# Moving the context projection of a second transformer block into the stream of expert weights

## The chip, the cores and the metric

The kernel runs on one core of a Trainium2 chip. It is one program for five engines: TensorE (PE, matrix products; PEld is its loading of weights), VectorE (DVE), ScalarE (ACT), GpSimd (POOL) and SyncE (SP), which here only starts transfers. The metric is the device time of one execution in microseconds (us).

## The reference

Two blocks run one after the other on 512 tokens of width 1024. The first one ends in a mixture of 16 experts, each of which takes 64 tokens; every expert has 24 MiB of weights in float32. The second block takes the normalized result x and a context of 256 tokens:

```python
x = x + ec_moe(rmsnorm(x, norm_ffn_g), router_w, expert_w_gu, expert_w_down)
x = rmsnorm(x, final_norm_g)
# second block; shift, scale, shift_c, scale_c come from c_2 and c_ctx_2
h  = rmsnorm_2(x, norm_g)   * (1 + scale)   + shift
hc = rmsnorm_2(ctx, norm_g) * (1 + scale_c) + shift_c
ckv, kr, kb, vb, cq, za, qb, zb, ga, gb = split_cols(h @ w_in, ...)   # 160 + 512 + 512 + 256 + ... columns
c_ckv, c_kr, c_kb, c_vb = split_cols(hc @ w_in[:, :1184], ...)        # the context projection
```

Then come a latent attention and a neighbourhood attention (tokens lie on 8 rows by 64 columns), both of which also attend to the context, gates, an output product, the residual and a last norm.

## The kernel before

**Experts.** Weights come from `in_expert_w_dram` as 192 ring tiles of [128, 4, 1024] (2 MiB), 12 for each expert, loaded by SP into a ring of nine slots (`Raw`: `first` fills the ring, `load` fetches one tile further each time one has been used). `expert(e, ...)` runs `up` four times and `down` twice. Between its parts it calls generators: `scatter(q)` adds the results of an expert pair to the residual `x` through one-hot matrices from `pick` (a comparison of `iota` with token numbers), `gather(q)` collects the next pair's tokens. For expert 15 the generator is `context()`.

**Before the experts**, `x` is complete after the last addition of the cross attention (L961), and the router takes its top 64 tokens in a chain of DVE instructions; `iota` is written by POOL at L1140, and the first `pick` (L1147) reads it.

**Context.** `context()` loads `ctx_2`, the two rows of gains, the context columns of `w_in_2` (`wkv`, 4 MiB in ring slots 2 and 3, and `wkr`), builds rows of shift and scale for the context and for x (`mod_rows`), normalizes the context (`mod_norm`) and transposes it into `hc`.

**Between the blocks.** After `scatter(7)`, `fin_norm(q)` takes two token tiles of 128 each: squares on ACT (L1418, L1420), the product with a gain (L1419), a Newton iteration of [128, 4] instructions on DVE (L143 to L162, L1423 to L1425), the scaled row h (L1429), the addition of the shift (L1431, one tile on DVE, one on POOL), then x itself is scaled on ACT (L1433). `fin_turn(t)` transposes h on PE and writes it as a high and a low part (L134 ACT, L135 DVE) into `hT`, in another token order (eight columns of the grid together). `ctx_proj(t)` multiplies `hc` by `wkv` and `wkr` and copies out (L1403, L1407). The first product of the second block, `pp`, is 416 columns wide (latent, rope and query latent): four weight units (L228 high part on ACT, L229 low part on DVE or POOL) in the outer loop and four token tiles in the inner one, three matrix products each (L129, L130, L131). `x` is kept in memory as `xd` meanwhile. At the end x comes back, and the output goes out in the plain token order, after `ymT` has been permuted back.

The order of instructions on each engine is set when the program is built, by a scheduler with a model of the times; on the chip each engine takes its queue in order.

Of the kernel before, what the change touches and what calls it, by code (L numbers as in the profile page):

```python
# [68 lines left out]
G_C, G_FFN = 25, 41  # L69
NCOL = 49  # L70
# [7 lines left out]
def body(ctx, tc, a, stop=None, dump=None):  # L78
# [819 lines left out]
    class Raw:  # L898
# [4 lines left out]

        def fetch(self, i):
            r, src = (i - len(self.specs)) % NW, self.specs[i]
            if r:
                w = slot(r, [128, 4, 1024], "we")
                nc.sync.dma_start(w, src)
                self.tiles[i] = [w[:, k] for k in range(4)]
                return  # L910

            self.tiles[i] = []
            for j in range(2):
                w = mid(("r8", "m8")[j], [128, 2, 1024], F32, "we")
                nc.sync.dma_start(w, src[:, 2 * j:2 * j + 2])
                self.tiles[i] += [w[:, 0], w[:, 1]]

        def first(self, r0, r1):
            for r in range(r0, r1):
                self.fetch((r + len(self.specs)) % NW)  # L920
# [6 lines left out]
        def use(self, i):  # L927

            return self.tiles.pop(i)

# [12 lines left out]
    wx = Raw([a["expert_w"][e, i] for e in range(16) for i in range(NT)])  # L943
# [156 lines left out]


# [42 lines left out]
    def pick(q, i):  # L1144

        o = p2("b2", [128, 512], F32R, "ot")
        V.tensor_scalar(o, iota, tokc[:, i, q:q + 1], None, op0=OP.is_equal)  # L1147
        return o

    def gather(q, n=4):  # L1150

        o = pick(q, 0)
# [19 lines left out]
    def scatter(q):  # L1172
        y = Y.pop(q)
        ot = [pick(q, i) for i in range(2)]
# [14 lines left out]
    def expert(e, mid_a, mid_b, half):  # L1189
        q, i = divmod(e, 2)  # L1190
        w0 = NT * e

        def up(j):
            p = ps(tag="gu")
            for k in range(8):
                if k % 4 == 0:
                    w = wx.use(w0 + 2 * j + k // 4)
# [3 lines left out]
                if k % 4 == 3:  # L1201
                    wx.load(w0 + 2 * j + k // 4 + 1 + NW)
# [18 lines left out]
        def down(c, hT, p):  # L1221
            for k in range(8):
                if k % 4 == 0:
                    w = wx.use(w0 + 8 + 2 * c + k // 4)
# [5 lines left out]
                if k % 4 == 3:  # L1230
                    wx.load(w0 + 8 + 2 * c + k // 4 + 1 + NW)
# [27 lines left out]
    def mod_rows(ab, v):  # L1259

        for i in range(2):
            for c in range(2):
                p = ps((128, 2, 256), tag="sc")
                for hf in range(2):
                    r = C_SEL + 32 * hf + 2 * (2 * i + c) + v
                    mm(p[:, hf], cst[:, r:r + 1].to_broadcast([128, 128]), mrow, True, True)
                d = ab[:, i, 512 * c:512 * c + 512]
                p = p.rearrange("p a b -> p (a b)")
                if i == 0:
                    S.activation(d, p, AF.Copy)  # L1270
                else:
                    V.scalar_tensor_tensor(d, p, 1.0, cx["g"][:, 0, 512 * c:512 * c + 512],
                                           op0=OP.add, op1=OP.mult)

    def mod_norm(src, ab, out):

        ss = sm.tile([128, 1], F32, name=nm("ss"), tag="ss1")
        S.activation(out, src, AF.Square, accum_out=ss)
        r = rsqrt(ss, 1024, 1, "mn")
        V.scalar_tensor_tensor(out, src, r, ab[:, 1], op0=OP.mult, op1=OP.mult)  # L1280
        G.tensor_add(out, out, ab[:, 0])

    def context():

        ctx_t = mid("b8", [128, 2, 1024], F32, "ctx")
        nc.sync.dma_start(ctx_t, a["ctx_2"][0].rearrange("(t p) d -> p t d", p=128))
        ga = slot(1, [128, 4, 1024], "gg")
        cx["g"], cx["ab"] = ga[:, 0:2], ga[:, 2:4]
        rows(cx["g"][:, 0], R_G2, 1024)
        rows(cx["g"][:, 1], R_FIN, 1024)  # L1290
        cx["kv"] = []
        for k in range(4):
            if k % 2 == 0:
                w4 = slot(2 + k // 2, [128, 4, 1024], "wkv")
            w = w4[:, 2 * (k % 2):2 * (k % 2) + 2]
            nc.sync.dma_start(w, w_in2[256 * k:256 * k + 256, 160:1184].rearrange("(k p) c -> p k c", p=128))
            cx["kv"].append(w)
        yield 1
        abc = mid("b8", [128, 2, 1024], F32, "abc")
        mod_rows(abc, 1)  # L1300
        mod_rows(cx["ab"], 0)
        yield 1
        hc = cx["hc"] = mid("r8", [128, 8, 256], F32, "hc")
        xn = mid("m8", [128, 2, 1024], F32, "xc")
        for t in range(2):
            mod_norm(ctx_t[:, t], abc, xn[:, t])
        yield 1
        for t in range(2):
            for j0 in (0, 4):
                p = ps((128, 4, 128), tag="tn")  # L1310
                for j in range(4):
                    T.transpose(p[:, j], xn[:, t, (j0 + j) * 128:(j0 + j + 1) * 128], ident)
                S.activation(hc[:, j0:j0 + 4, tsl(t)], p, AF.Copy)
        w = cx["kr"] = mid("m8", [128, 8, 160], F32, "wkr")
        nc.gpsimd.dma_start(w, w_in2[:, 0:160].rearrange("(k p) c -> p k c", p=128))
# [6 lines left out]
    for e in range(NEX):  # L1322
# [24 lines left out]
    p3 = Pool("p3", "left", {"b8": 4, "w4": P3W, "h4": P3H, "b4": 2, "ck": 1})  # L1347
# [45 lines left out]
    ckr = p3("ck", [128, 2, 160], F32, "ckr")  # L1393
    ckb = p3("b4", [128, 2, 512], F32, "ckb")
    cvb = p3("b4", [128, 2, 512], F32, "cvb")

    def ctx_proj(t):
        act = lambda k: cx["hc"][:, k, tsl(t)]
        for i, dst in enumerate((ckb, cvb)):
            p = ps(tag="cx")  # L1400
            for k in range(8):
                mm(p, act(k), cx["kv"][k // 2][:, k % 2, 512 * i:512 * i + 512], k == 0, k == 7)
            S.activation(dst[:, t], p, AF.Copy)  # L1403
        p = ps(tag="cx")
        for k in range(8):
            mm(p[:, :160], act(k), cx["kr"][:, k], k == 0, k == 7)
        S.activation(ckr[:, t], p[:, :160], AF.Copy)  # L1407
# [3 lines left out]
    def fin_norm(q):  # L1411
# [23 lines left out]
    def fin_turn(t):  # L1435
        h = hn2[t // 2][:, t % 2]
        for i in range(2):
# [3 lines left out]
            hh, hl = hT.buf(i)  # L1441
# [11 lines left out]
    xd = ctx.enter_context(tc.tile_pool(name="dram", bufs=1, space=bass.MemoryType.DRAM)).tile(  # L1453
        [128, 4, 1024], F32, name="xd")
# [598 lines left out]
```

## Time and profile before

| | us |
|---|---|
| median of 3 runs (lowest, highest) | 1931.11 (1928.12, 1932.21) |
| the profiled execution, whole | 1936.54 |
| its span in the trace | 1933.6 |

Times in the rows count from the start of the span. In a timeline row stand the start, the duration, the engine, the line, the operation with its output and inputs, a count, and in brackets how long the engine had been idle and what ended that.

### The profile page before, as it was taken

How to read it: one execution, taken by the hardware profiler on the slowest of the kernel's cores; microseconds unless marked ns; L12 is line 12 of the kernel's file. 1: busy time of each engine (PE TensorE's matmuls, PEld its weight loads, DVE VectorE, ACT ScalarE, POOL GpSimd, SP SyncE). 2: the span in 40 equal slices, each digit the busy share in tenths (PEclk: the TensorE clock that was granted, in tenths of full speed). 3: DMA queues.
4: the chain of work that ended last, by engine and by line, in shares of the span. 5: the costliest groups of instructions: out<-in, count | busy, mean ns of one | idle time of the engine just before them, and what ended most of it. 6: DMA issues, size and time to landing. Idle time of an engine off the chain costs nothing.

```text
span 1933.6 us, 24628 instructions
## 1 busy us (share of the span) xinstructions
PE 1750.2 (91%) x10248; PEld 1085.2 (56%) x10248; DVE 681.6 (35%) x1364; ACT 491.5 (25%) x946; POOL 256.1 (13%) x271
## 2 busy tenths in 40 slices
PE   6999999969999898878888798887899999999998
PEld 6975579943433232323323233322487888888778
DVE  6696786540011101001020010101634333554565
ACT  4335543411000000000000000001445444344433
POOL 2371102000000000000000000001213111333351
PEclk9998999979999999999999999999999999999999
DMA  6322623449999999999999999999322202332232
GB/s 213 110 80 85 205 76 95 175 184 409 426 427 425 425 427 426 425 427 426 426 426 426 427 425 425 428 425 416 108 69 61 55 23 58 88 96 82 80 112 85
DMA packets 95870, 493.33 MB, mean 255 GB/s; under 512 B 6484, under 2 KB 56384, under 8 KB 68112
## 3 DMA queue, kind: packets, MB, share of 16 engines
q1 hardware_dynamic: 91008, 475.49, 61.9%
q0 software_dynamic: 3168, 10.45, 1.8%
q10 hardware_dynamic: 1584, 5.83, 0.8%
q8 instruction: 80, 1.31, 0.3%
q14 instruction: 30, 0.25, 0.0%
HBM read 486.50 MB, written 4.19 MB: 254 GB/s over the span
## 4 chain that ended last, share of the span: by engine, by line
PE 47%; DMA 40%; DVE 3%; ACT 1%; issue 1%; POOL 0%; ACTq 0%; SPq 0%; DVEq 0%
DMA we<-in_expert_w_dram 39%; PE ps L126 18%; PE ps L129 8%; PE ps L130 8%; PE ps L131 8%; PE ps L1652 1%; PE ps L1810 1%; PE ps L743 1%; DMA w<-in_w_out_dram 1%; DMA voff<-vb 1%; DVE wl L229 0%; PE ps L1629 0%; PE ps L1216 0%; DVE x L1419 0%; PE ps L1779 0%
## 5 line engine op out<-in xcount | busy, mean ns | idle before, releaser
L126 PE MATMUL ps<-we,xe 128*64 128x512 f32 x2048 | 465.2, 598 | 57.7 <-DMA we<-in_expert_w_dram 57.7
L126 PEld LDWEIGHTS ps<-we,xe 128*64 128x64 f32 x2048 | 143.3, 137 | 346.6 <-issue 258.2
L126 PE MATMUL ps<-we,hT 128*64 128x512 f32 x1024 | 236.3, 604 | 28.3 <-DMA we<-in_expert_w_dram 23.0
L126 PEld LDWEIGHTS ps<-we,hT 128*64 128x64 f32 x1024 | 71.7, 138 | 164.1 <-issue 133.9
L228 ACT ACTIVATE wh<-w 128x1024 fp32r<-128x1024 f32 (+4 forms) x100 | 103.8, 1040 | 122.8 <-PE ps L130 74.0
L1252 DVE SCALAR_TENSOR_TENSOR y<-ps,gate,y 64x512 fp32r<-64x512 f32 x32 | 23.9, 748 | 308.8 <-ACT y L1251 308.8
L1210 DVE TENSOR_TENSOR hid<-hid,ps 128x512 f32<-128x512 f32 x32 | 22.0, 688 | 310.7 <-PE ps L126 291.0
L1218 ACT ACTIVATE hT<-ps 128x512 f32<-128x512 f32 x32 | 19.1, 597 | 430.2 <-PE ps L1216 430.2
L229 POOL TENSOR_TENSOR wl<-w,wh 128x1024 fp32r<-128x1024 f32 (+2 forms) x38 | 90.2, 2375 | 264.3 <-ACT wh L228 241.7
L300 POOL DMA_DIRECT2D gg<-in_rows_dram x2 | 1.1, 560 | 899.0 <-DMA we<-in_expert_w_dram 899.0
L229 DVE TENSOR_TENSOR wl<-w,wh 128x1024 fp32r<-128x1024 f32 (+3 forms) x58 | 77.9, 1344 | 72.3 <-ACT wh L228 71.9
L1251 ACT ACTIVATE y<-ps,gate 64x512 fp32r<-64x512 f32 x32 | 21.8, 682 | 249.5 <-PE ps L126 238.7
L129 PE MATMUL ps<-hTh,wh 128*128 128x512 f32 x192 | 77.3, 403 | 1.6 <-ACT va L1567 1.6
L130 PE MATMUL ps<-hTl,wh 128*128 128x512 f32 x192 | 76.4, 398 | 0.0
L131 PE MATMUL ps<-hTh,wl 128*128 128x512 f32 x192 | 76.1, 397 | 0.0
L126 PEld LDWEIGHTS ps<-otT,xn 128*128 128x128 f32 x512 | 61.0, 196 | 24.6 <-issue 23.6
L129 PE MATMUL ps<-wh,hTh 128*128 128x256 f32 (+1 forms) x224 | 67.1, 299 | 1.2 <-ACT hTh L134 1.0
L126 PE MATMUL ps<-otT,xn 128*128 128x128 f32 x512 | 66.9, 286 | 0.7 <-ACT otT L1157 0.7
L130 PE MATMUL ps<-wl,hTh 128*128 128x256 f32 (+1 forms) x224 | 66.3, 296 | 0.0
L131 PE MATMUL ps<-wh,hTl 128*128 128x256 f32 (+1 forms) x224 | 65.5, 295 | 0.0
L1169 DVE TENSOR_TENSOR xe<-ps,cols 128x512 f32<-128x512 f32 (+1 forms) x18 | 10.2, 598 | 148.9 <-PE ps L126 148.9
L1181 DVE TENSOR_TENSOR x<-x,ps 128x512 f32<-128x512 f32 x64 | 41.8, 685 | 57.7 <-PE ps L126 57.7
(560 smaller groups left out, 3362.7 us busy)
## 6 DMA issues: line engine op xcount, KB each, us to landing
we<-in_expert_w_dram SPq DMA_DIRECT2D x171, 2048.0 KB, 34.4
we<-in_expert_w_dram SPq DMA_DIRECT2D x42, 1024.0 KB, 34.4
w<-in_w_in_dram SPq DMA_DIRECT2D x48, 512.0 KB, 3.7
w<-in_w_mod_dram SPq DMA_DIRECT2D x24, 512.0 KB, 4.3
w<-in_w_out_dram SPq DMA_DIRECT2D x16, 512.0 KB, 3.7
w<-in_ca_wkv_dram SPq DMA_DIRECT2D x8, 512.0 KB, 5.1
wkv<-in_w_in_dram SPq DMA_DIRECT2D x4, 1024.0 KB, 32.0
bm<-in_bias_dram POOLq DMA_DIRECT2D x16, 256.0 KB, 3.7
```

The costliest lines, as they stand in the source:

```text
L126: T.matmul(out, l, r, start=st, stop=sp)
L129: T.matmul(out, L[0], R[0], start=st, stop=False)
L130: T.matmul(out, L[0], R[1], start=False, stop=False)
L131: T.matmul(out, L[1], R[0], start=False, stop=sp)
L228: S.activation(h, w, AF.Copy)
L229: (G if (self.ns % 3 == 2 if self is ws else W3E(self.ns)) else V).tensor_sub(l, w, h.bitcast(F32))
L743: T.transpose(pp[:, j], st[u][hf][:, tsl(j)], ident)
L1181: V.tensor_add(xs, xs, p)
L1210: V.tensor_mul(h, h, pu)
L1251: S.activation(Y[q][r, 2 * d], p[r], AF.Copy, scale=g)
L1252: V.scalar_tensor_tensor(Y[q][r, 2 * d + 1], p[r], g, Y[q][r, 2 * d].bitcast(F32), op0=OP.mult, op1=OP.subtract)
L1652: T.transpose(p[:, j], P[:, tsl(c0 + j)], ident)
```

## The change

- The context comes as four further ring tiles between those of experts 9 and 10 (`CE = 10`, `NC = 4`): `ctx_2`, `ctx_kr` and two halves of `ctx_kv`, laid out for it in memory. A slot is now given on by `done(i)`, in whatever order tiles are finished.
- After expert 9, `ctx_norm()` normalizes and transposes the context, with shift and scale as columns (`mod_cols`), and `ctx_proj()` computes all of its products and writes the result to memory (`cxd`, `crd`) on the POOL queue. It is read back after the experts.
- `context()` goes. For expert 15 there is `before()`: gains, one row of scale, a load `w_lat` of the four weight units of the first product, and their split into high and low parts, the low parts on DVE.
- `x` is written to memory and read back in the grid order ahead of the experts, on the POOL queue; `scatter` uses `iotb`, a second iota in that order. `hT` and `ymT` are then written without permutation, and each output transfer takes 64 partitions.
- `fin_norm` no longer adds the shift; `fin_turn` adds it as a bias of each [128, 128] block, and the products of a token tile follow its `fin_turn` at once.

```diff
+            self.slot = {i: (i + 2) % NW for i in range(NW)}
         def fetch(self, i):
-            r, src = (i - len(self.specs)) % NW, self.specs[i]
+            r, src = self.slot[i], self.specs[i]
...
-        def load(self, upto):
-            while self.nl < min(upto, len(self.specs)):
+        def done(self, i):
+            if self.nl < len(self.specs):
+                self.slot[self.nl] = self.slot[i]
                 self.fetch(self.nl)
                 self.nl += 1
...
+    wx = Raw([a["expert_w"][e, i] for e in range(CE) for i in range(NT)]
+             + [flat(a["ctx_2"]), flat(a["ctx_kr"]), flat(a["ctx_kv"][0]), flat(a["ctx_kv"][1])]
+             + [a["expert_w"][e, i] for e in range(CE, 16) for i in range(NT)])
...
     for r in FO:
         wx.first(r, r + 1)
+    dram = ctx.enter_context(tc.tile_pool(name="dram", bufs=1, space=bass.MemoryType.DRAM))
+    xo = dram.tile([4, 128, 1024], F32, name="xo")
+    nc.gpsimd.dma_start(xo.rearrange("t p d -> p t d"), x)
+    xv = xo.rearrange("t p d -> (t p) d").rearrange("(r b c) d -> b r c d", r=8, c=8)
+    for b in range(8):
+        nc.gpsimd.dma_start(x[64 * (b % 2):64 * (b % 2) + 64, b // 2], xv[b])
...
     iota = p2("b2", [128, 512], F32, "iota")
+    iotb = p2("b2", [128, 512], F32, "iotb")
     G.iota(iota, pattern=[[1, 512]], base=0, channel_multiplier=0, allow_small_or_imprecise_dtypes=True)
+    G.iota(iotb, pattern=[[8, 8], [64, 8], [1, 8]], base=0, channel_multiplier=0, allow_small_or_imprecise_dtypes=True)
...
+    def ctx_norm():
+        mod_cols()
+        w = cx["w"] = wx.use(NT * CE)
+        c, hc = w[:, 0:2], w[:, 2:4].rearrange("p a b -> p (a b)").rearrange("p (k n) -> p k n", k=8)
         for t in range(2):
+            r = rsqrt(sumsq(c[:, t], w[:, 2 + t]), 1024, 1, "cr")
+            S.activation(c[:, t], c[:, t], AF.Copy, scale=r)
+        for t in range(2):
             for j0 in (0, 4):
                 p = ps((128, 4, 128), tag="tn")
                 for j in range(4):
+                    T.transpose(p[:, j], c[:, t, (j0 + j) * 128:(j0 + j + 1) * 128], ident)
+                for j in range(4):
+                    k = j0 + j
+                    V.tensor_scalar(hc[:, k, tsl(t)], p[:, j], mcol[:, 1, 1, k:k + 1], mcol[:, 1, 0, k:k + 1],
+                                    op0=OP.mult, op1=OP.add)
+    def ctx_proj():
+        c, hc = cx["c"], cx["hc"]
+        for i in range(2):
+            w = wx.use(NT * CE + 2 + i).rearrange("p a b -> p (a b)").rearrange("p (k c) -> p k c", k=8)
+            for t in range(2):
+                p = ps(tag="sc")
+                for k in range(8):
+                    mm(p, hc[:, k, tsl(t)], w[:, k], k == 0, k == 7)
+                S.activation(c[:, t, 512 * i:512 * i + 512], p, AF.Copy)
+            wx.done(NT * CE + 2 + i)
...
+        nc.gpsimd.dma_start(crd, kr)
+        wx.done(NT * CE + 1)
+        nc.gpsimd.dma_start(cxd, c)
+        wx.done(NT * CE)
+    def before():
+        ga = slot(1, [128, 4, 1024], "gg")
...
+        w = slot(2, [128, 8, 416], "wlat")
+        nc.sync.dma_start(w, a["w_lat"])
...
+        for u, (hu, lu) in enumerate(cx["lat"]):
+            wu = w[:, 2 * u:2 * u + 2]
+            S.activation(hu, wu, AF.Copy)
+            V.tensor_sub(lu, wu, hu.bitcast(F32))
...
         else:
-            ga = context()
+            ga = before()
             expert(e, lambda n: None, lambda n: run(ga, 2), lambda: None)
+        if e == CE - 1:
+            ctx_norm()
+            ctx_proj()
...
+    nc.gpsimd.dma_start(ckb, cxd[:, :, 0:512])
+    nc.gpsimd.dma_start(cvb, cxd[:, :, 512:1024])
+    for u in range(4):
+        w3.parts[u] = cx["lat"][u]
+    w3.nl = w3.ns = 4
...
-            V.scalar_tensor_tensor(h[:, i], x[:, 2 * q + i], rr[:, i:i + 1], cx["ab"][:, 1],
-                                   op0=OP.mult, op1=OP.mult)
-            (G if i else V).tensor_add(h[:, i], h[:, i], cx["ab"][:, 0])
+            V.scalar_tensor_tensor(h[:, i], x[:, 2 * q + i], rr[:, i:i + 1], cx["a"], op0=OP.mult, op1=OP.mult)
...
-            for r in range(2):
-                src = p[:, :, 64 * r:64 * r + 64].rearrange("p k (b c) -> p k b c", c=8)
-                d = [v.rearrange("p k (b r c) -> p k b r c", r=8, c=8)[:, :, :, 2 * t + r] for v in (hh, hl)]
-                evac_hl(d[0], d[1], src)
+            hh, hl = hT.blk(i, 0, 4, tsl(t))
+            for j in range(4):
+                b = mcol[:, 0, 0, 4 * i + j:4 * i + j + 1]
+                S.activation(hh[:, j], p[:, j], AF.Identity, bias=b)
+                V.scalar_tensor_tensor(hl[:, j], p[:, j], b, hh[:, j].bitcast(F32), op0=OP.add, op1=OP.subtract)
+    pp = [ps(tag="pp") for _ in range(4)]
     for q in range(2):
         fin_norm(q)
     for t in range(4):
         fin_turn(t)
-    for t in range(2):
-        ctx_proj(t)
+        for u in range(4):
+            h, l = w3.get(u)
+            for k in range(2):
+                mm3(pp[t][:, :416], hT(2 * u + k, tsl(t)), (h[:, k], l[:, k]), u + k == 0, u == 3 and k == 1)
+    w3.ahead(6)
...
-    G.tensor_copy(tck[:, 4:6], ckr)
+    nc.gpsimd.dma_start(tck[:, 4:6], crd)
...
-        nc.scalar.dma_start(a["out"][0, tsl(t), :512], x[:, t, :512])
-        nc.sync.dma_start(a["out"][0, tsl(t), 512:], x[:, t, 512:])
+        for b in range(2):
+            o = a["out"][0].rearrange("(r b c) d -> b r c d", r=8, c=8)[2 * t + b]
+            (nc.scalar, nc.sync)[b].dma_start(o, x[64 * b:64 * b + 64, t])
```

## Rows read from the trace of the kernel before

**Rows 1.** The page: PE's busy time, and the chain that ended last.

```profile
PE 1750.2 (91%) x10248; PEld 1085.2 (56%) x10248; DVE 681.6 (35%) x1364; ACT 491.5 (25%) x946; POOL 256.1 (13%) x271
...
PE 47%; DMA 40%; DVE 3%; ACT 1%; issue 1%; POOL 0%; ACTq 0%; SPq 0%; DVEq 0%
```

**Rows 2.** Stretches: length, busy time by engine, PE clock, DMA share, GB/s.

```profile
418.00:433.00 15.00, 14.44 (x74) 8.86 (x75) 0.87 (x3) 1.25 (x3) 0.00 (x0) 0.85 0.00 1
...
600.00:1000.00 400.00, 346.75 (x1626) 128.83 (x1624) 49.54 (x78) 26.70 (x44) 0.00 (x0) 1.00 1.01 426
...
1363.00:1387.00 24.00, 17.17 (x58) 9.00 (x57) 22.11 (x37) 12.96 (x20) 11.58 (x5) 0.96 0.24 69
1387.00:1409.00 22.00, 21.43 (x72) 11.74 (x72) 5.26 (x14) 6.67 (x19) 1.98 (x3) 0.89 0.20 83
1409.00:1428.00 19.00, 18.43 (x98) 18.27 (x99) 4.33 (x8) 7.13 (x24) 1.97 (x1) 1.00 0.24 70
```

**Rows 3.** Timeline of PE in expert 14: one ring tile of 16 products.

```profile
1284.00 3.65 PE L126 MATMUL ps<-we,hT 128*64 128x512 f32 x16 [1.16 <-DMA we<-in_expert_w_dram]
```

**Rows 4.** Timeline of SP's transfers at the end of the experts.

```profile
1301.23 7.72 SPq L908 DMA_DIRECT2D we<-in_expert_w_dram  x3
1317.20 19.15 SPq L1296 DMA_DIRECT2D wkv<-in_w_in_dram  x4
```

**Rows 5.** Timeline of PE from the last expert tile to the first product.

```profile
1348.07 0.20 PEld L126 LDWEIGHTS ps<-we,hT 128*64 128x64 f32 x4 [0.71 <-DMA we<-in_expert_w_dram]
...
1363.05 13.90 PE L126 MATMUL ps<-wkv,hc 128*128 128x512 f32 x32
...
1376.78 1.04 PE L1440 MATMUL ps<-cst,h 128*128 128x128 f32 x8
1377.71 2.44 PE L126 MATMUL ps<-wkr,hc 128*128 128x160 f32 x16
1386.98 9.59 PE L126 MATMUL ps<-wkv,hc 128*128 128x512 f32 x16 [6.83 <-ACT cvb L1403]
...
1397.29 7.03 PE L126 MATMUL ps<-wkv,hc 128*128 128x512 f32 x16
...
1427.60 0.35 PE L131 MATMUL ps<-wh,hTl 128*128 128x416 f32 x1
```

**Rows 6.** Timeline of DVE and POOL in the same stretch.

```profile
1356.84 1.31 DVE L1181 TENSOR_TENSOR x<-x,ps 128x512 f32<-128x512 f32 x2 [0.26 <-PE ps L126]
...
1366.88 4.09 POOL L229 TENSOR_TENSOR wl<-w,wh 128x832 fp32r<-128x832 f32 x2 [7.06 <-ACT wh L228]
...
1367.18 1.92 DVE L1423 TENSOR_SCALAR fnv<-fss 128x2 f32<-128x2 f32 x1
...
1382.19 2.48 DVE L1429 SCALAR_TENSOR_TENSOR h<-x,fnr,gg 128x1024 f32<-128x1024 f32 x2
...
1387.24 1.63 DVE L135 TENSOR_TENSOR hTl<-ps,hTh 128x256 fp32r<-128x256 f32 x4 [1.43 <-ACT hTh L134]
```

**Rows 7.** Transfers: output, input, queue, count, KB each, median us to landing.

```profile
we<-in_expert_w_dram SPq DMA_DIRECT2D x171, 2048.0 KB, 34.4
...
xd<-x ACTq DMA_DIRECT2D x1, 2048.0 KB, 6.3
...
voff<-vb POOLq DMA_DIRECT2D x2, 512.0 KB, 10.1
out_dram<-x ACTq DMA_DIRECT2D x4, 256.0 KB, 2.5
```

**Rows 8.** Timeline of DVE and POOL ahead of the experts.

```profile
395.26 0.69 DVE L961 TENSOR_TENSOR x<-x,ps 128x512 f32<-128x512 f32 x1 [1.58 <-PE ps L131]
...
413.14 0.56 POOL L1140 IOTA iota<- 128x512 f32 x1 [84.92 <-DVE bidx L1113]
...
416.16 0.49 DVE L1147 TENSOR_SCALAR ot<-iota,tokc 128x512 fp32r<-128x512 f32 x1
```

**Rows 9.** Instructions of a line: count, then ns shortest, median and longest.

```profile
L1419 DVE TENSOR_TENSOR x<-x,gg x4: 1218/1219/1225, 1360.0 to 1366.0; 128x1024 f32<-128x1024 f32 x4
```

More of the change, by code (lines that the diff above doesn't have):

```diff
@@ L919, in first, with use, rows @@
             for r in range(r0, r1):
-                self.fetch((r + len(self.specs)) % NW)
-        def load(self, upto):
-            while self.nl < min(upto, len(self.specs)):
+                self.fetch((r - 2) % NW)
+        def use(self, i):
+            return self.tiles.pop(i)
+        def rows(self, i):
+            w = self.use(i)
+            return w if isinstance(w, list) else [w[:, k] for k in range(4)]
+        def done(self, i):
+            if self.nl < len(self.specs):
+                self.slot[self.nl] = self.slot[i]
                 self.fetch(self.nl)
                 self.nl += 1
-        def use(self, i):
-            return self.tiles.pop(i)
     class QParts:
@@ L1173, in scatter @@
         y = Y.pop(q)
-        ot = [pick(q, i) for i in range(2)]
+        ot = [pick(q, i, iotb) for i in range(2)]
         for t in range(4):
@@ L1196, in up @@
                 if k % 4 == 0:
-                    w = wx.use(w0 + 2 * j + k // 4)
+                    w = wx.rows(w0 + 2 * j + k // 4)
                 for t in range(2):
@@ L1201, in up @@
                 if k % 4 == 3:
-                    wx.load(w0 + 2 * j + k // 4 + 1 + NW)
+                    wx.done(w0 + 2 * j + k // 4)
                 if j == 0 and k % GN == GN - 1:
@@ L1230, in down @@
                 if k % 4 == 3:
-                    wx.load(w0 + 8 + 2 * c + k // 4 + 1 + NW)
+                    wx.done(w0 + 8 + 2 * c + k // 4)
         pg = up(0)
@@ L1257, in body @@
     cx = {}
[L1259 to L1304, printed above, removed]
@@ new lines, in body, with mod_cols @@
+    mcol = gts.rearrange("p a b -> p (a b)")[:, 0:32].rearrange("p (v i k) -> p v i k", v=2, i=2)
+    def mod_cols():
+        p = ps((128, 2, 64), tag="sc")
+        for s in range(2):
+            mm(p[:, s, :40], mrow[:, tsl(s)], cst[:, C_SEL:C_SEL + 40], True, True)
+        pv = p.rearrange("p s (h x) -> p s h x", h=2)
+        for v in range(2):
+            for i in range(2):
+                d = mcol[:, v, i].rearrange("p (c h s) -> p s h c", c=2, h=2)
+                src = pv[:, :, :, 4 * i + v:4 * i + v + 3:2]
+                for s in range(2):
+                    if i == 0:
+                        V.tensor_copy(d[:, s], src[:, s])
+                    else:
+                        g = cols[:, G_2:G_2 + 8].rearrange("p (c h s) -> p s h c", c=2, h=2)
+                        V.scalar_tensor_tensor(d[:, s], src[:, s], 1.0, g[:, s], op0=OP.add, op1=OP.mult)
@@ L1489, in keys_b @@
             w3.ahead(x0 + 2 + t0 // 2)
-    pp = [ps(tag="pp") for _ in range(4)]
-    for u in range(4):
-        h, l = w3.get(u)
-        for t in range(4):
-            for k in range(2):
-                mm3(pp[t][:, :416], hT(2 * u + k, tsl(t)), (h[:, k], l[:, k]), u + k == 0, u == 3 and k == 1)
-        w3.ahead(u + 2)
     keys_b(0, X_KB, CT)
@@ L2024, in layout @@
     out["expert_w"] = out["expert_w"].reshape(16, 12, 128, 4, 1024)
+    w2 = A["w_in_2"][0].reshape(8, 128, -1).transpose(1, 0, 2)
+    out["ctx_2"] = A["ctx_2"][0].reshape(2, 128, 1024).transpose(1, 0, 2)
+    out["ctx_kv"] = np.stack([w2[:, :, 160:672], w2[:, :, 672:1184]])
+    out["ctx_kr"] = w2[:, :, 0:160]
+    out["w_lat"] = np.concatenate([w2[:, :, 0:160], w2[:, :, 1184:1440]], axis=2)
     u = A["w_ukv_2"][0].reshape(128, 8, 2, 64).transpose(0, 2, 1, 3)
```

85 lines of the change are left out of this document (46 added, 39 removed).

## The prediction

> **What bounds the kernel now.** I read the page first. PE is busy 91% of the span, yet the chain that ended last is only 47% PE and 40% DMA [rows 1]: a long stage waits for transfers. The stretches say which. From 600 to 1000 us the transfers run at 426 GB/s with their engines fully busy, while PE has 13% of its time over [rows 2]. A ring tile of 2 MiB (2.097 MB) takes 2.097/0.426 = 4.92 us to arrive, and its 16 products take 3.65 us, after which PE waits [rows 3]. So in the expert stage every byte ahead of the last expert tile counts at 426 GB/s, and PE work is free as long as it fits into the spare time and the ring never stands full. Two ends of this stage matter. Ahead of it, from 418 to 433 us, the transfers stand still at 1 GB/s: the ring is full, and PE has not yet freed a tile [rows 2]. Behind it, the context weights `wkv` are queued after the last expert tiles [rows 4], so their 4 MiB delay no expert.
>
> The second thing is the joint between the blocks. The last expert tile is there at 1348.07; the first product of the second block ends at about 1427.8 [rows 5]. That is 79.7 us, in which PE's own work is not the only limit. From 1363 to 1387 DVE is busy 22.1 of 24 us with the norm [rows 2], and PE fills this time with half of the context projection (32 products in 13.9 us). The other half begins at 1386.98, after 6.83 us of waiting for an ACT copy that stood in ACT's queue behind the scaling of x; its 16 products then take 9.59 us where the last 16 take 7.03, and the clock granted in that stretch is 0.89, not 1.00 [rows 2, 5]. Only then, from about 1409.5, comes the first product with 18.4 us of PE [rows 2].
>
> **The change part by part.** *More bytes ahead of the last expert tile.* The two halves of `ctx_kv` are 4.19 MB, `ctx_kr` 0.66 MB; the result written to memory is 1.05 + 0.16 MB. `ctx_2` was ahead of the last expert tiles before. Together 6.06 MB, at 0.426 MB/us: +14.2 us. Nothing hides this, because the transfers have no gap from 433 us on. If stores cost more than loads, the bound is the row of `xd<-x`, 2.10 MB in 6.3 us to landing [rows 7], a rate of 0.333, and 1.21 MB then take 3.6 instead of 2.8: +15.0.
>
> *The block of work after expert 9.* Its norm is a chain over ACT, DVE and PE, some 12 us as an estimate (two squares and two scalings at about 1.1 us, as long as a [128, 1024] instruction here, two Newton chains of about 2.4 us, DVE's share of the transposes). Then 32 products of 512 columns and 16 of 160: 13.9 + 2.4 = 16.3 us [rows 5], with a clock loss of 9.59 - 7.03 = 2.6 us after an idle PE. Expert 10 so starts about 31 us after the end of expert 9. Does the ring run dry? Nine tiles are issued ahead: the four of the context, then five of expert 10, about 35 us of transfer from the end of expert 9. The first slot comes free when one `ctx_kv` half is done, after 12 + 7 + 2.6 = 22 us, the second after 29; the two that wait for the store come after some 35. No gap: 0 us. PE itself is then some 16 us late, since expert 10's first tile landed at 15 us. It gains at least (4.92 - 3.65) less its gathers and scatters, in the mean 13% of 59 us, or some 6 to 7 us, on each expert; six experts follow, so it has caught up before expert 15. Taken: 0, bounds 0 and +8.
>
> *The reordering of x.* 2.1 MB out and 2.1 MB in on POOL's queue, 9.8 us at 426 GB/s. x is complete at 396 us [rows 8], the standstill lasts until 433 [rows 2], and what it delays are ring tiles that PE needs only after two others. So its bytes cost 0, with the standstill as cover; without it, 9.8 us. But POOL's queue has `iota` behind these nine issues, eight of which wait for the first to land. Before, `iota` runs at 413.14 and `pick` needs it at 416.16 [rows 8]: 2.5 us to spare. If the first transfer takes 10 us beside the ring's, the last issue is at about 413 to 416. A delay here is paid in full, since PE's first freed tile restarts the transfers. Taken +1, bounds 0 and +8.
>
> *The joint.* Working from the landing of the last tile: its products take 3.6 us; the weighted copies 2.2, no longer interleaved with the rows of `mod_rows` and with context transposes; 5.8. Eight additions of 0.65 and four products with the gain at 1.22 ran as one DVE chain in 10.4 us and will again [rows 6, 9]: 16.2. Then twice a Newton chain and two h rows: each chain is some 2.4 us when undisturbed, the rows 2.5 us [rows 6]. Undisturbed is new: now a 0.16 us instruction takes 1.92 us at 1367.18, while POOL runs its L229 [rows 6], and three others like it fall beside POOL's work on weights and shift. Both POOL jobs go. So 16.2 + 2 x 4.9 = 26.0, plus the four low parts of `w_lat`, now on DVE, about 1.0 each: 30. Turning the first token tile: eight transposes, eight copies of 128 columns, for which 0.29 us each on DVE is my estimate (0.41 for 256 columns [rows 6]); 32.5. From here PE has 18.1 us of products and 16 more transposes in 2.1 [rows 2, 5], while DVE with 32 x 0.29 = 9.3 stays ahead: 52.7. A cold start costs 2.6 as above: 55.3. If the scheduler turns the first half as soon as its h is there (at 21), this becomes 47. I take 53, near the upper end, because DVE before turned nothing until the second half's h was through (1387.24 after 1384.7 [rows 6]). Gain: 79.7 - 53 = 26.7, bounds 24 and 33. What follows is not changed in its order: the key product still stands between the first product and the norm that needs the context's part, and covers the read of `crd`; its two weight units have ACT and DVE nearly free.
>
> *Output.* Each half now needs both ACT's and DVE's half of the row, and 64 partitions take part. The row of before is 2.5 us for 256 KB; the only 64-partition transfer is `voff<-vb`, 10.1 us for 512 KB [rows 7]. Bounds 0 and +5; taken +1, near the row of the same direction. [...]
>
> *Sum.* +14.2 + 0 + 1 - 26.7 + 1 = -10.5. The profiled execution's 1936.54 us (span 1933.6) becomes 1926; it lies 5.4 above the median of the runs, so for the median 1931.1 - 10.5 = 1920.6, say 1921.
>
> **The rivals.** *First: POOL's queue holds up the start.* If `iota` lands behind reads that wait for the store of x, expert 0 starts later and the whole stream with it: 416 + 8 instead of 416, so 1921 + 7 = 1928. For it speaks that eight issues of about half a microsecond and a store in competition must fit into 17 us; against it that the scheduler may put `iota` first, which waits only for a buffer. [...]
>
> *Second, on the other side: the first product finds no cover.* The split of `w_lat` cannot begin before its load, which stands behind the last expert tile. If the scheduler queues it wrongly (ACT's four high parts ahead of the weighted copies, DVE's low parts behind the norms), the products start only after all turning, at 30 + 10 + 3 = 43, and end at 43 + 18 + 2.6 + the stall of about 4 in front = 68. The gain is then 12, and the sum +14.2 + 1 - 12 + 1 = +4.2: 1935.3, slower. It decides where the first product ends later than 53 + 10.5 = 63.5 us after the last tile. For it: ACT's queue already showed such a stall (6.83 us [rows 5]). Against it: the four units were split in time before.
>
> *Third: more than forecast.* The first half is turned early and x's detour costs nothing: -33 + 14.2 + 0.5 = -18, or 1913.
>
> *Fourth: the ring stands full* after expert 9, or PE is still late at the end: +8 to +15 on the forecast, 1929 to 1936.
>
> **How the numbers follow.** Forecast (1915 to 1927) 0.48; first rival (about 1928) 0.14; second (about 1935.3) 0.16; third (about 1913) 0.14; fourth 0.08. Measurements of this kernel can tell 0.2% (3.9 us) from no change, so faster means under 1927.2, slower over 1935. Faster: 0.48 + 0.14 + a third of the first rival, 0.05 = 0.67. Same: the rest of the first, half of the second and of the fourth: 0.20. Slower: 0.13. The range that leaves out 2 in 10 reaches beyond the times of the third rival and of the second: 1909 to 1936; the forecast's own is 1915 to 1927.
>
> **What would show it.** Right: the last expert tile lands 14 to 17 us later than at 1348; the transfers stay at 426 GB/s through the stretch after expert 9; no projection of the context behind expert 15; the first product ends 47 to 56 us after the last tile; the 0.16 us instructions of the norm never take 1.9 us. Wrong: a gap in the transfers after expert 9, an `iota` later than 416, PE without waits for ring tiles in expert 15, or a first product that starts after the last token tile is turned.

## The result and the profile after

The changed kernel takes 1954.17 us (median of 4 runs, 1952.35 to 1958.1) against 1931.66 for the kernel before: a ratio of 1.0119, 95% interval 1.0095 to 1.0144. It is slower; 1921 was forecast, with a range from 1909 to 1936. Its profiled execution takes 1953.79 us, its span 1952.1. The medians lie 22.5 us apart and the two spans 18.5, mostly because the profiled execution of the kernel before (1936.54) is 4.9 above its median.

Between executions the stages ahead of the experts end up to 10 us apart, so stretches are compared from an anchor: the PE transposes of the router's result. First the kernel before, timeline of PE: this anchor and the transposes of the query latent behind the joint.

```profile
413.92 0.72 PE L1125 MATMUL ps<-cst,both 48*128 48x48 f32 x2 [11.88 <-DVE both L1121]
...
1439.30 1.04 PE L1529 MATMUL ps<-cst,tcq 128*128 128x128 f32 x8
```

The same of the changed kernel, with its first transposes of `ot`, its last expert tile, the turning of its first token tile (the row at 1402.46) and the end of its first product (the row at 1438.19).

```profile
412.67 0.72 PE L1149 MATMUL ps<-cst,both 48*128 48x48 f32 x2 [11.52 <-DVE both L1145]
427.15 1.08 PE L1181 MATMUL ps<-cst,ot 128*128 128x128 f32 x4 [13.76 <-DVE ot L1173]
...
1377.93 3.65 PE L126 MATMUL ps<-we,hT 128*64 128x512 f32 x16 [1.16 <-DMA we<-in_expert_w_dram]
...
1402.46 1.94 PE L1491 MATMUL ps<-cst,h 128*128 128x128 f32 x8 [6.90 <-DVE h L1481]
...
1438.19 0.35 PE L131 MATMUL ps<-wlh,hTl 128*128 128x416 f32 x1
...
1452.54 1.97 PE L1576 MATMUL ps<-cst,tcq 128*128 128x128 f32 x8 [12.45 <-DVE tcq L1552]
```

With the last DVE instruction (L1949 before, 1928.87 + 0.75; L1994 after, 1944.47 + 0.75) the whole difference falls into five stretches. The last column is the repaired version with the lowest ratio, from the experiments below.

| stretch, us | before | changed | difference | forecast | repaired (`e10`) |
|---|---|---|---|---|---|
| anchor to last expert tile | 934.2 | 965.3 | +31.1 | +15.2 | 948.6 |
| to the end of the first product | 79.9 | 60.6 | -19.3 | -26.7 | 54.2 |
| to the transposes of the query latent | 11.4 | 14.0 | +2.6 | 0 | 13.7 |
| to the end of DVE's last instruction | 490.3 | 492.7 | +2.4 | 0 | 492.0 |
| to the end of the span | 4.0 | 6.9 | +2.9 | +1 | 6.8 |

The differences add up to 19.7; the anchor itself is 1.2 earlier, which gives the 18.5 between the spans. (Four profiles of kernels that leave the first stretch alone give 963.0 to 965.3 for it.)

Four things ask for a cause. The first is the start. Timeline of POOL in the changed kernel:

```profile
395.22 0.81 POOL L1119 DMA_DIRECT2D xo<-x  x1 [68.31 <-DVE lt L1075]
...
420.68 4.44 POOL L1122 DMA_DIRECT2D x<-xo  x8 [24.32 <-DMA xo<-x]
425.06 0.65 POOL L1165 IOTA iota<- 128x512 f32 x1
```

POOL waits 24.3 us for the write of x before it can issue the reads, and `iota` stands behind them: 425.06 instead of 413.14 [rows 8]. The second is the transfers. Stretches of the changed kernel, columns as in [rows 2]:

```profile
396.00:418.00 22.00, 2.54 (x25) 1.22 (x23) 15.03 (x69) 2.85 (x9) 0.36 (x2) 0.61 1.01 415
418.00:433.00 15.00, 5.11 (x22) 4.50 (x24) 1.56 (x2) 0.80 (x2) 6.04 (x10) 0.50 0.72 196
433.00:438.00 5.00, 5.00 (x26) 2.36 (x24) 0.29 (x1) 0.21 (x2) 0.00 (x0) 0.82 0.00 0
438.00:443.00 5.00, 5.00 (x28) 2.37 (x26) 0.29 (x1) 0.69 (x2) 0.00 (x0) 1.00 0.26 52
...
1020.00:1040.00 20.00, 20.00 (x52) 7.82 (x51) 0.45 (x2) 1.79 (x3) 0.00 (x0) 1.00 0.98 415
1040.00:1060.00 20.00, 20.00 (x89) 9.63 (x89) 1.12 (x2) 1.80 (x4) 1.16 (x2) 1.00 0.79 306
```

The standstill that ended at 433 before [rows 2] now ends at about 442, and behind expert 9 there is a new gap: 306 instead of 426 GB/s over 20 us is 5.6 us lost, while PE has no idle time. What SP's queue waited for between 1020 and 1060 us (total, times, longest) is PE alone:

```profile
SPq L913 <- PE ps L126: 28.1, 4, 15.4
SPq L920 <- PE ps L126: 13.4, 2, 10.7
```

The third is the 12.45 us for which PE waits ahead of the query latent's transposes; before it did not wait there at all. The fourth is the 2.4 us in the second block. Stretches from these transposes to the end of DVE's last instruction, and their first 7 us, before and then changed:

```profile
1439.30:1929.62 490.32, 476.54 (x3280) 404.61 (x3278) 243.17 (x405) 212.22 (x407) 140.24 (x124) 0.99 0.26 75
1439.30:1446.30 7.00, 6.21 (x42) 5.78 (x40) 3.27 (x5) 3.67 (x6) 0.00 (x0) 1.00 0.60 153
```

```profile
1452.54:1945.22 492.68, 479.08 (x3278) 408.26 (x3278) 239.69 (x402) 210.35 (x404) 141.92 (x124) 0.98 0.25 72
1452.54:1459.54 7.00, 7.00 (x27) 6.58 (x28) 1.50 (x2) 1.38 (x2) 0.00 (x0) 0.56 0.00 0
```

PE waits no longer in this block than before (13.6 us against 13.8). The same products take it 2.5 us more, at a lower granted clock: behind the wait of 12.45 us it is granted 0.56 of full speed for 7 us, where it had 1.00.

### The profile page after: what moved, and what is told of

Same layout as the page of the kernel before. It is cut to its first block, busy times and chain, and to the rows that moved or that the text cites. A ratio compares the mean times of both kernels' runs of the same rounds, so it can differ in the third digit from the quotient of the medians.

```text
span 1952.1 us, 24641 instructions
## 1 busy us (share of the span) xinstructions
PE 1753.4 (90%) x10228; PEld 1091.4 (56%) x10228; DVE 679.7 (35%) x1402; ACT 495.4 (25%) x956; POOL 247.2 (13%) x276
## 4 chain that ended last, share of the span: by engine, by line
PE 53%; DMA 29%; issue 4%; DVE 2%; ACT 2%; POOL 1%; DVEq 0%; ACTq 0%; SPq 0%; POOLq 0%
PE ps L126 28%; DMA we<-in_expert_w_dram 25%; PE ps L129 7%; PE ps L130 7%; PE ps L131 6%; DMA we<-in_ctx_kr_dram 1%; DMA xo<-x 1%; PE ps L1699 1%; PE ps L743 1%; PE ps L1857 1%; DMA voff<-vb 1%; PE ps L1242 0%; ACT wh L228 0%; DVE wl L229 0%; DVE x L1207 0%
## 5 line engine op out<-in xcount | busy, mean ns | idle before, releaser
L228 ACT ACTIVATE wh<-w 128x1024 fp32r<-128x1024 f32 (+3 forms) x96 | 100.2, 1046 | 120.4 <-PE ps L130 76.1
L229 POOL TENSOR_TENSOR wl<-w,wh 128x1024 fp32r<-128x1024 f32 (+1 forms) x34 | 83.2, 2447 | 250.4 <-ACT wh L228 250.2
L229 DVE TENSOR_TENSOR wl<-w,wh 128x1024 fp32r<-128x1024 f32 (+3 forms) x58 | 75.3, 1299 | 66.7 <-ACT wh L228 62.1
L126 PE MATMUL ps<-y,ot 128*128 128x512 f32 x128 | 45.3, 450 | 13.3 <-DVE x L1207 8.8
L129 PE MATMUL ps<-wh,hTh 128*128 128x256 f32 x192 | 56.2, 293 | 0.1
L130 PE MATMUL ps<-wl,hTh 128*128 128x256 f32 x192 | 55.6, 289 | 0.0
```

What stands on the lines that cost most here:

```text
L126: T.matmul(out, l, r, start=st, stop=sp)
L129: T.matmul(out, L[0], R[0], start=st, stop=False)
L130: T.matmul(out, L[0], R[1], start=False, stop=False)
L228: S.activation(h, w, AF.Copy)
L229: (G if (self.ns % 3 == 2 if self is ws else W3E(self.ns)) else V).tensor_sub(l, w, h.bitcast(F32))
```

## The experiments

**One: iota ahead of the reads of x.**

```diff
-    for b in range(8):
-        nc.gpsimd.dma_start(x[64 * (b % 2):64 * (b % 2) + 64, b // 2], xv[b])
...
+    with tc.issue_after(nc.cur_bb.bb.instructions[-1]):
+        for b in range(8):
+            nc.gpsimd.dma_start(x[64 * (b % 2):64 * (b % 2) + 64, b // 2], xv[b])
```

> The changed kernel, but POOL issues the eight reads of x only behind the two iotas; the write of x stays where it was. Theory: the start was lost because iota stood behind reads that waited 24.3 us for the write. Then iota runs at about 413 to 414, PE's transposes of ot start at 416 to 418 instead of 427.15, the transfers start again near 433 and the last expert tile is used 10 to 12 us earlier than 1377.93: 1366 to 1368. Time 1954 - 11 = 1943 (1941 to 1945). Rival: the 4.2 MB of the detour itself delay ring tiles that PE needs. Then the last expert tile moves by less than 3 us and the time stays at 1951 to 1954.

Ratio to before 1.0065 (1.0044 to 1.0086), 1945.83 us. Timeline of POOL, then of PE (the anchor in two rows, the transposes of `ot`, the last expert tile):

```profile
400.43 0.81 POOL L1119 DMA_DIRECT2D xo<-x  x1 [68.31 <-DVE lt L1075]
...
417.32 0.56 POOL L1163 IOTA iota<- 128x512 f32 x1 [15.76 <-DVE bidx L1135]
...
424.31 4.48 POOL L1167 DMA_DIRECT2D x<-xo  x8 [5.17 <-DMA xo<-x]
```

```profile
418.10 0.31 PE L1147 MATMUL ps<-cst,both 48*128 48x48 f32 x1 [11.87 <-DVE both L1143]
...
421.74 1.09 PE L1182 MATMUL ps<-cst,ot 128*128 128x128 f32 x4 [2.14 <-DVE ot L1174]
...
1370.80 3.65 PE L126 MATMUL ps<-we,hT 128*64 128x512 f32 x16 [1.16 <-DMA we<-in_expert_w_dram]
```

From the anchor, the transposes of `ot` come after 3.6 us instead of 14.5, and the last expert tile after 952.7 us instead of 963.0 to 965.3. The write of x still takes as long (23.3 us to landing, 24.9 in the changed kernel), and it does no harm: the theory holds, and the order on POOL's queue cost some 11 us by the traces (7 to 10 by the ratios). The bytes of the detour are hidden as forecast: 952.7 is 18.5 above the kernel before, which the other bytes (14.2) and the gap behind expert 9 (322 GB/s for 20 us here, 4.9 us) fill. (The absolute times of the expectation missed, because the anchor came 5.4 us later in this execution.)

**Two: the key product behind the first product.** `cx["last"]` is the last PE instruction of the first product; `issue_after` puts instructions of an engine behind a given one on its queue.

```diff
-    keys_b(0, X_KB, CT)
+    with tc.issue_after(cx["last"]):
+        keys_b(0, X_KB, CT)
```

> The changed kernel, with the key product (the one of 256 columns) held on PE behind the last instruction of the first product. Theory: the hole of 12.45 us before the transposes of the query latent is there because the key product, which covered the norm chain before, was used up between the token tiles. Held back, the first product ends 49 to 53 us after the last expert tile instead of some 62, the hole shrinks to under 3 us, and the time falls by 9 to 11 us: 1944 (1942 to 1946). Rival: the chain waits for something else (the weights of the next product, the read of the context's result), or the first product is held by the turning of the tiles anyway: hole stays over 8 us and the time within 3 us of 1954.

Ratio 1.0076 (1.0057 to 1.0095), 1947.37 us. Timeline of PE: last expert tile, turning of the first token tile, end of the first product, transposes of the query latent.

```profile
1375.95 3.65 PE L126 MATMUL ps<-we,hT 128*64 128x512 f32 x16 [1.17 <-DMA we<-in_expert_w_dram]
...
1400.50 1.94 PE L1491 MATMUL ps<-cst,h 128*128 128x128 f32 x8 [6.91 <-DVE h L1481]
...
1427.67 0.35 PE L131 MATMUL ps<-wlh,hTl 128*128 128x416 f32 x1
...
1443.42 1.94 PE L1578 MATMUL ps<-cst,tcq 128*128 128x128 f32 x8 [3.89 <-DVE tcq L1554]
```

The first product ends 52.1 us after the last tile (60.6), and the hole falls from 12.45 to 3.89. From the last tile to the transposes it is 67.5 us instead of 74.6, a gain of 7.1; by the ratios (1.0076 against 1.0119, and 1.0099 when the changed kernel ran again as `e8`) it is 4 to 8. The theory holds, though 9 to 11 were expected: ACT now stood 4.9 us in front of a copy of the key product before it could square the last two token tiles.

**Three: half of the projection's products, same transfers.** The output of this kernel lacks the projection of the context's second half.

```diff
-            for t in range(2):
+            for t in range(1):
                 p = ps(tag="sc")
                 for k in range(8):
...
```

The rope part is halved in the same way (not shown).

> The changed kernel with the context projection done for the first 128 context tokens only (the other half keeps other numbers): the same transfers, half of PE's products after expert 9. Theory: the projection is 64 products of 512 columns and 32 of 160, some 35 us of PE, twice what was counted, and the transfers stop at 1040 because PE has not given enough tiles back. With half of it the stretch 1040 to 1060 goes back to 420 to 428 GB/s, the last expert tile comes 5 to 6 us earlier (1372 to 1373), time 1948 to 1949. Rival: the slots that wait for the two stores hold SP's queue; then the gap stays, perhaps earlier, and the time stays at 1952 to 1954.

Ratio 1.0089 (1.0070 to 1.0108), 1950.21 us. Stretches:

```profile
1020.00:1040.00 20.00, 20.00 (x85) 8.24 (x85) 2.57 (x4) 1.70 (x4) 1.16 (x2) 1.00 1.01 427
1040.00:1060.00 20.00, 15.55 (x72) 5.58 (x68) 3.17 (x5) 1.20 (x2) 0.00 (x0) 0.95 1.01 428
```

The gap is gone with the stores still in place; the last expert tile comes 958.9 us after the anchor, 4 to 6 us earlier. Half the products also let the store of the result leave earlier, so this run alone does not clear the store; but in the changed kernel SP's queue waited for PE alone through the gap (above), and it went on at 1044.66, ahead of the store at 1045.6. So it is PE's work that kept slots from coming free. Groups of PE by shape, 1000 to 1060 us of the changed kernel, say how much work:

```profile
L126 PE MATMUL ps<-we,we 128*128 128x512 f32 x64 | 30.9, 639 | 0.0
...
L126 PE MATMUL ps<-we,we 128*128 128x160 f32 x32 | 4.8, 302 | 0.0
L1319 PE MATMUL ps<-cst,we 128*128 128x128 f32 x16 | 3.7, 389 | 5.2 <-ACT we L1314 4.5 <-DVE we L1322 0.7
```

64 products and 32, not the 32 and 16 of the forecast: the loops of `ctx_proj` make 32 and 16 calls, and the trace has two instructions for each.

**Four: output by 128 partitions.** Rows of the output land in the wrong places.

```diff
-        for b in range(2):
-            o = a["out"][0].rearrange("(r b c) d -> b r c d", r=8, c=8)[2 * t + b]
-            (nc.scalar, nc.sync)[b].dma_start(o, x[64 * b:64 * b + 64, t])
+        nc.scalar.dma_start(a["out"][0, tsl(t), :512], x[:, t, :512])
+        nc.sync.dma_start(a["out"][0, tsl(t), 512:], x[:, t, 512:])
```

> The changed kernel with the output written by 128 partitions and half rows as before (the rows land in the wrong order). From the last instruction on DVE to the end of the span it was 4.0 us before and is 6.9 us now. Theory: that is the pattern of 64 partitions; the end shrinks by 2.5 to 3 us, time 1951 to 1951.5. Rival: it is only that both halves must be complete before the transfer starts: the tail stays over 6 us, time within 1 us of 1954.

Ratio 1.0086 (1.0066 to 1.0106), 1950.58 us. From DVE's last instruction (1948.45 + 0.75) to the end of the span (1953.2) it is 4.0 us again. Stretches around it, first the changed kernel, then this one:

```profile
1944.00:1946.00 2.00, 0.00 (x0) 0.00 (x0) 1.13 (x3) 0.72 (x1) 0.00 (x0) 0.50 0.45 164
...
1948.00:1949.00 1.00, 0.00 (x0) 0.00 (x0) 0.00 (x0) 0.00 (x0) 0.00 (x0) 0.50 0.43 156
1949.00:1950.00 1.00, 0.00 (x0) 0.00 (x0) 0.00 (x0) 0.00 (x0) 0.00 (x0) 0.50 0.52 193
```

```profile
1948.00:1950.00 2.00, 0.00 (x0) 0.00 (x0) 1.13 (x3) 0.72 (x1) 0.00 (x0) 0.93 0.00 0
1950.00:1951.00 1.00, 0.00 (x0) 0.00 (x0) 0.00 (x0) 0.00 (x0) 0.00 (x0) 0.50 0.94 358
```

With 64 partitions the share of busy DMA engines stays at about a half (0.43 to 0.52), with 128 it reaches 0.94. While DVE is still at its last instructions, the transfers of the token tile before are on their way in the changed kernel (0.45) and done in this one (0.00). The edit also lets each half of the row leave without the other; `e9` below does that with 64 partitions, and it does not help.

**Five to eight: the repairs together.** `e5` has one and two, and ACT's copies of the key product held behind its squares. `e6` also cuts the projection in two pieces, three experts apart (`CE, CF = 9, 12`):

```diff
         if e == CE - 1:
             ctx_norm()
-            ctx_proj()
+            ctx_proj(0)
+            ctx_rope()
+        if e == CF - 1:
+            ctx_proj(1)
+            nc.gpsimd.dma_start(cxd, cx["c"])
+            wx.done(X_C)
```

`e7` is `e6` with `G.tensor_sub` in place of `V.tensor_sub` for the low parts of `w_lat`; `e8` is the changed kernel again.

> The changed kernel with the two repairs of the first experiments together (iota ahead of the reads of x; key product behind the first product on PE), and the copies of the key product on ACT behind the squares and copies that the norm of the query latent needs. Theory: two separate losses, so the gains add: -10.4 and -8.3 by the ratios, and the 3.9 us hole that was left before the transposes of the query latent (ACT stood behind a key copy for 4.9 us) goes too: 1954 - 22 = 1932, a ratio to the kernel before of 0.998 to 1.002. From the last expert tile to these transposes 63 to 65 us (67.5 with the keys behind alone). Rival: the gains overlap or the hole has another cause; 1936 to 1940, ratio over 1.002.

> As the run with both repairs, and the context projection cut in two: its norm, the first half of its columns and the rope part behind expert 9's place one expert earlier (behind expert 8), the second half of the columns behind expert 11; same bytes, same products. Theory: the transfers stopped because 43 us of PE work in one piece is more than nine slots carry; in two pieces of some 27 and 14 us nothing stops, every stretch from 480 to the last expert tile shows 420 us or more GB/s, and the last expert tile is used 934.2 + 14.2 = 948 to 949 us after the transposes of the router's result, where it was 965.3 in the changed kernel and 952.7 with iota first. Time 4 to 5 us below the run with both repairs: 1927 to 1928, ratio 0.996 to 0.998. Rival: the slot that holds the context for three experts, or the store behind which SP's queue stands, brings the gap back: last tile 951 or more, time as with both repairs.

> As the run with the projection in two, with the low parts of w_lat on POOL instead of DVE. Theory: the four subtractions of 1.0 us stand in DVE's chain between the additions to x and the weighted copies; without them the first product ends 2 to 4 us earlier (48 to 50 us after the last expert tile) and the time falls by 2 to 4 us. Rival: POOL's work makes DVE's small instructions beside it slow, as one of 0.16 us took 1.92 before, or DVE would have waited for PE there anyway: first product within 1 us of the run before it, time the same or up to 3 us more.

> The changed kernel once more, unaltered, on the same chip as the three other runs, so that they can be compared with it directly. All theories: 1952 to 1956, ratio to the kernel before 1.010 to 1.014.

| | median us | ratio to before (95%) | anchor to last tile | to first product's end | wait for query latent |
|---|---|---|---|---|---|
| `e5` | 1936.47 | 1.0012 (0.9996 to 1.0028) | 952.4 | 54.2 | 2.94 |
| `e6` | 1933.33 | 1.0012 (0.9994 to 1.0031) | 950.1 | 52.8 | 2.94 |
| `e7` | 1934.59 | 1.0013 (0.9997 to 1.0029) | 950.5 | 54.3 | 2.94 |
| `e8` | 1953.9 | 1.0099 (1.0083 to 1.0116) | 963.4 | 60.5 | 12.51 |

`e5` is 17 us below `e8`, about what the traces of one and two gave apart (11 and 7), and not the 22 expected, so it lies between theory and rival: a wait of 2.94 stays, and from the last tile to the transposes of the query latent it is 68.6 us instead of 63 to 65. `e6` shortens the first stretch by 2.3 of the 4 to 5 us; 372 GB/s are left at 1000 to 1020. The ratios do not tell `e5` from `e6`, so the 1927 to 1928 expected did not come. In `e7` the rival was right on the time, and the first product ends 1.5 us later instead of earlier. Timeline of DVE while POOL works 8.72 us on the low parts:

```profile
1379.34 2.77 DVE L1479 TENSOR_TENSOR x<-x,gg 128x1024 f32<-128x1024 f32 x1
...
1382.63 2.36 DVE L1479 TENSOR_TENSOR x<-x,gg 128x1024 f32<-128x1024 f32 x1
...
1385.59 1.21 DVE L1479 TENSOR_TENSOR x<-x,gg 128x1024 f32<-128x1024 f32 x1
```

The product with the gain takes 2.77 and 2.36 us beside POOL and 1.21 after it: 2.7 us lost of the 4 that the four moved subtractions took on DVE. One more low part of later weights (L229, 1.2 us) stands in its chain than in `e6`. The first token tile is turned 25.5 us after the last expert tile, against 24.7 in `e6`.

**Nine to eleven: balance, output halves, and the price of a byte.** `e10` moves the rope part into the second piece and holds the keys' norm chain on DVE behind the query latent's scaling; `e9` also cuts each output transfer into two half rows. `e11` is the kernel before with extra ring transfers that nothing reads:

```diff
-    wx = Raw([a["expert_w"][e, i] for e in range(16) for i in range(NT)])
+    wx = Raw([a["expert_w"][e, i] for e in range(10) for i in range(NT)]
+             + [a["expert_w"][9, i][:, 0:1] for i in range(9)]
+             + [a["expert_w"][e, i] for e in range(10, 16) for i in range(NT)])
```

> As the next run, and each output transfer of 64 partitions cut into two halves of the row: the first half, which ACT has ready, goes first, so that only the second is left when DVE has written its part. Theory: the tail of 6.9 us from DVE's last instruction shrinks to 4.5 to 5.5 us, 1.5 to 2.5 us below the next run. Rival: it is the pattern of 64 partitions that is slow, or the number of transfers; the tail stays over 6.3 us.

> As the projection in two, with the rope part moved to the second piece (22 and 19 us of PE instead of 27 and 14), and the norm chain of the keys' latent held on DVE behind the scaling of the query latent. Theory: the 372 GB/s of 1000 to 1020 us go back to 424, so the last expert tile is used 948 to 949 us after the transposes of the router's result instead of 950.1; the hole of 2.94 us before the transposes of the query latent falls under 1 us. Time 3 to 4.5 us below the projection in two (1933.3): 1929 to 1930, a ratio of 0.996 to 0.999. Rival: the gap comes from the held slot and the store and stays, and the keys' norm only moves into the way of the next products: time within 1.5 us of 1933.

> The kernel before, with nine further transfers of 0.52 MB each (4.72 MB of expert 9's weights, read again and not used) in the ring between experts 9 and 10, and nothing else. Theory: a byte ahead of the last expert tile costs 1/426 us per kB whatever it is for: 4.72 / 0.426 = 11.1 us; the last expert tile is used 945.2 us after the transposes of the router's result (934.15 before), time 1934 + 11 = 1945, ratio 1.005 to 1.007. Rival: part of it is hidden, or small transfers keep the ring short: under 7 us or over 14 us.

`e11`: the last tile is used at 1362.76, 945.1 us after its anchor at 417.70, that is 10.9 later than before, for 11.1 expected; the ratio is 1.0076 (1.0051 to 1.0101), with 1.005 to 1.007 expected. `e10`: 1933.48 us, ratio 0.9990 (0.9975 to 1.0006); the last tile 948.6 after the anchor as expected, every stretch from 453 us to the last tiles at 420 GB/s or more. But the time stayed at that of `e6` instead of 1929 to 1930, as its rival had it, and the wait for the query latent is still 2.19. Timeline of DVE ahead of that wait, inside the norm chain of the query latent:

```profile
1430.11 0.96 DVE L229 TENSOR_TENSOR wl<-w,wh 128x768 fp32r<-128x768 f32 x1 [2.47 <-ACT wh L228]
...
1433.82 0.96 DVE L229 TENSOR_TENSOR wl<-w,wh 128x768 fp32r<-128x768 f32 x1 [2.68 <-ACT wh L228]
```

Two low parts of later weights stand in front of the rest of the chain on DVE's queue, and DVE waits 2.47 and 2.68 us for their high parts; holding them behind the chain was not tried. `e9`: 1933.98, ratio 0.9998 (0.9983 to 1.0013); its tail, from DVE's last instruction to the end of the span, is 7.8 us, and the share of busy DMA engines is 0.49 from 1925 to 1930 us, so cutting the transfers does not help, and the rival was right. (12 of its 16 transfers stand on ACT's queue, so the tail is not that of the cut alone.)

**Twelve: only half of the projection moved.** The keys' columns are loaded last and computed after `scatter(7)`:

```diff
+             + [a["expert_w"][e, i] for e in range(CE, 16) for i in range(NT)] + [flat(a["ctx_kv"][0])])
...
     run(scatter(7))
+    ctx_proj(0)
+    nc.gpsimd.dma_start(cxd[:, :, 0:512], cx["c"][:, :, 0:512])
```

> As the balanced run, but only half of the projection is moved: in one piece behind expert 11 the norm, the rope part and the columns of the values; the columns of the keys' part (2.1 MB) are loaded behind the last expert tile, and their products fill PE between the scatter of the last expert pair and the first turned token tile, where it waits for the norm on DVE. Bytes ahead of the last expert tile: 2.10 + 0.66 + 0.68 stored = 3.44 MB instead of 6.06. Theory: a byte ahead of the last tile costs 1/426 us per kB and PE's wait behind it is free, so the last expert tile is used 934.2 + 8.1 = 942 us after the transposes of the router's result (948.6 in the balanced run), the first product ends within 2 us of the balanced run's 54 us after the last tile, and the time falls by 4 to 7 us: 1927 to 1930, ratio 0.995 to 0.998. Rival: the 13.9 us of products do not fit under the norm and push the first product back by as much as the bytes gave; first product 58 us or more after the last tile, time as the balanced run, 1932 to 1935.

1943.1 us, ratio 1.0038 (1.0022 to 1.0055): worse than `e10`. Timeline of SP, then of PE:

```profile
1328.59 0.33 SPq L911 DMA_DIRECT2D we<-in_ctx_kv_dram  x1
1334.58 0.33 SPq L913 DMA_DIRECT2D we<-in_expert_w_dram  x1
```

```profile
1383.79 16.15 PE L126 MATMUL ps<-we,we 128*128 128x512 f32 x32
1399.77 1.04 PE L1497 MATMUL ps<-cst,h 128*128 128x128 f32 x8
```

SP issued the keys' columns ahead of the last expert tile, so their bytes were paid after all (949.0 us from the anchor instead of 942). And the products ran from 20.6 to 36.6 us after the last tile and pushed the first turned token tile from 24.6 to 36.6; the first product ended at 65.8. The rival's mechanism held, with a time above the 1932 to 1935 that it gave. What the order of the loads alone cost was not tried apart.

## Why the prediction was wrong

- **More bytes, +14.2: right.** `e11` pays 10.9 us for 4.72 MB (11.1 by the same price), and `e10`, without gaps, is 14.4 above before in the first stretch.
- **The block after expert 9, 0 with bounds 0 and +8: the step "32 products of 512 columns and 16 of 160: 13.9 + 2.4 = 16.3 us" failed.** [rows 5] holds three rows of this product, 32, 16 and 16; only the first was counted, although the prediction itself calls these 32 half of the projection. The block is 35.7 us of products, PE gave slots back too late, and the transfers lost some 5 us (`e3`). That is the mechanism of the fourth rival, at less than its +8; it lies inside the bounds of the term.
- **The reordering of x, +1 with bounds 0 and +8: the step "if the first transfer takes 10 us" failed.** It took 24.9, beside the ring tiles in flight (share of busy DMA engines 1.01 from 396 to 418 us), and landed at 420.1, when the engines ran out of work (0.91 from 418 to 420 us, 0.08 from 420 to 421). That its bytes hide was right (`e1`); the first rival, `iota` behind the reads, came true with 11 us instead of 7.
- **The joint, -26.7.** The 53 us from the last tile to the end of the first product came out in `e2`, 52.1, but by luck. The forecast had the first token tile turned behind all of the norm, at about 30 us. It was turned at 24.5, in the changed kernel and in `e2`, which is the condition of the third rival, priced at 47: the turning began 3.5 us later than the 21 assumed there, and the rest took 27.5 us instead of 26. (The sum there counts 16 further transposes, 2.1 us; three token tiles have 24.) The step that failed is "What follows is not changed in its order: the key product still stands between the first product and the norm". The scheduler filled PE's waits between turned token tiles with the key product, so the first product ended at 60.6 and nothing was left to cover the norm chain (12.45 us of wait). Of 26.7 us, 16.7 came. The second rival's point, 63.5 us, was not reached.
- **Output, +1 with bounds 0 and +5: a size,** 2.9 measured. The transfers from 64 partitions to 8 grid rows kept about half of the DMA engines busy (share 0.43 to 0.52, against 0.94 from 128 partitions in `e4`); no run tells the 8 rows from the 64 partitions. The +1, taken near the row of 2.5 us for 256 KB, was too little, as the transfers of the tile before were also still on their way (share 0.45 while DVE was at its last instructions).
- **+2.4 in the second block** was not foreseen. The prediction put nothing there; the trace shows the same products at a lower granted clock (0.56 for the first 7 us), and no run tried it apart.

Together +14.2 + 5 + 11 - 16.7 + 2.9 + 2.4 = 18.8, for 18.5 between the spans, instead of -10.5. The range failed because the rivals were taken as alternatives: the first and the mechanism of the fourth came together, and a step outside all of them, the cover of the norm chain, went as well. With these repaired the change is about even (`e10`, 0.9990): 14.4 us of bytes ahead of the last tile against 18.8 gained behind it, and the difference is no more than the measurement tells.

## What to carry to other kernels

Take the amount of a moved piece of work from a view that groups by shape, since a timeline splits it into several rows. Where an engine's queue holds an instruction that waits for a transfer, charge everything behind it with that wait as it is beside full DMA engines (here 24.9 us for 2 MB, not 10), and put what the next stage needs ahead of it. Work that covers a wait stays there only if something holds it: when a new wait opens earlier, a scheduler can spend the cover there, as this one did. A number that comes out is no proof of the steps behind it: check the path too.

## What the runs showed of the hardware

A write of 2 MB on POOL's queue took 24.9 us to land in the changed kernel, 23.3 in `e4` and 23.3 in `e1`, where the iotas no longer stood behind the reads that wait for it; meanwhile SP's ring loads kept the DMA engines full (share 1.01 from 396 to 418 us in the changed kernel). At the 426 GB/s of 600 to 1000 us its bytes alone would be 4.9 us, as an estimate. The output transfers from 64 partitions to 8 grid rows ran at about half of the DMA engines (share 0.43 to 0.52, against 0.94 from 128 partitions in `e4`), and cutting them in two did not raise that (0.49 in `e9`). A DVE instruction of 1.21 us took 2.77 beside POOL's subtractions in `e7`. Behind a wait of 12.45 us PE was granted 0.56 of its clock over 7 us in the changed kernel, and eight transposes took 1.97 us where they had taken 1.04 in the kernel before.
